# A small load by GpSimd ahead of everything, and two transposing turns placed differently, in a two-matmul kernel with a GELU between

## The chip, the core and the metric

The kernel runs on one core of one Trainium2 chip. The metric is the device time of one execution in microseconds. Before the change three runs gave 117.18, 117.56 and 117.73 us; the median is 117.56.

The engines go by the names of the profile: PE is TensorE (matmuls; PEld is its loading of weights), DVE is VectorE, ACT is ScalarE, POOL is GpSimd, SP is SyncE. SP, ACT and POOL also issue DMA transfers; the profile calls the queue of SP's transfers q1, that of POOL's q0, that of ACT's q10.

## The reference

```python
m, k, n, p = 1024, 1024, 2048, 1024          # a: m x k, b: k x n, c: n x p, all float32

def reference(a, b, c):
    h = np.matmul(a, b)
    h = 0.5 * h * (1 + np.tanh(np.sqrt(2 / np.pi) * (h + 0.044715 * h ** 3)))
    return np.matmul(h, c).astype(np.float32)
```

## The kernel before, in words

**The work.** The kernel computes the first product transposed: a tile of 128 columns of b as weights, the transposed a as the moving operand, so that a result is h transposed (hT, 16 tiles of 128 rows, in two halves of 512 columns: half 0 for the upper 512 rows of a, half 1 for the lower). The first four tiles (columns 0 to 511 of b) are summed over eight steps of 128 along k, both halves side by side. All that remains is done as three groups of block products, seven for each two-by-two product of blocks (`seven`, `product`, line 212): `zero` for columns 512 to 1023 of b, `one` for columns 1024 to 2047, `two` for the second matmul. GELU runs on ACT on the way from PSUM to hT.

**Loads.** SP loads the first pieces in float32 (lines 75 to 79): columns 0 to 255 of a's upper rows (`sta[:, 0, 0]`), rows 0 to 255 of b's first 512 columns (`stb[:, 0:2]`), columns 0 to 255 of a's lower rows (`sta[:, 1, 0]`), columns 256 to 511 of a's upper rows (`sta[:, 0, 1]`), rows 256 to 383 of b (`stb[:, 2]`). DVE and ACT cast these to bf16 (`cast_a`, `cast_b`). POOL loads all the rest with the cast to bf16 in the transfer (lines 91 to 104): the other quarters of a (`abq`, four row tiles by 256 columns), the rest of b, and c. Before the first of these it copies one element per partition of the first piece of a to `gate` (line 81), so that its transfers are issued only after that piece has landed. POOL's transfers use eight completion semaphores in turn: each from the ninth on waits for the one eight before it.

**Turns.** a must be transposed on PE. A turn (line 138) takes one quarter of one half of a, 512 rows by 256 columns. It goes in two parts, one for each 128 columns: four transposes of 128x128 into a half of a PSUM bank, then a DVE copy of 128x512 to `aT` (line 146). As a generator it stops after each part, so that matmuls can be placed between them. Given one bank, both parts use it, and the second part's transposes wait for the first part's copy; given two banks, each part has its own.

**The order of work.** It is written out by hand, and each engine runs its instructions in that order. PE begins with throwaway float32 matmuls (`stir`). Then come the turn of the first upper quarter (0, 0), with the first two steps along k of the upper half (`block(0, ...)`), the turn of the first lower quarter (1, 0), the first two steps of the lower half, the turn (0, 1) and so on, a turn between every two or so blocks, each using what has just landed. The lower half has only three of its four result tiles in that loop, since the banks are taken; the fourth (`ps[1, 3]`, bank 7) is summed after the upper half's end. The last turn, of the last lower quarter (1, 3), stands among the matmuls of this fourth tile. Behind it come steps 6 and 7 of the lower half, then `zero`.

The places that the change touches are lines 51 to 55 (the identity for the transposes, `gate`, `g`, and a tile `room` that nothing uses), lines 237 to 242 (the first lower quarter's cast and turn) and lines 272 to 278 (the fourth tile and the last turn). `cast_a` (line 128) splits a quarter's 256 columns over the engines it is given; a pair in its place casts two row tiles each on the two engines of the pair.

Of the kernel before, what the change touches and what calls it, by code (L numbers as in the profile page):

```python
# [9 lines left out]
F32 = mybir.dt.float32  # L10
# [9 lines left out]
def kernel(ctx, tc, a, b, c, out):  # L20
    nc = tc.nc
    M, K = a.shape
    _, N = b.shape
    _, P = c.shape
# [5 lines left out]
    bv = b.rearrange("(kt p) n -> p kt n", p=128)  # L30
# [3 lines left out]
    consts = ctx.enter_context(tc.tile_pool(name="consts", bufs=1))  # L34
# [5 lines left out]
    def slot(tag, shape, dt, name):  # L40
        return big.tile(shape, dt, name=name, tag=tag)

    def bank(i, shape=(128, H), dt=F32, name="ps"):
        return pp.tile(list(shape), dt, name=name, tag=f"bank{i}", padded_shape=None)

    def pieces(tag, bufs, shape, dt, name):
        return small.tile(shape, dt, name=name, tag=tag, bufs=bufs)

    warm = nc.const_aps.tensor(0.0, [128, 256], F32)
    ident = consts.tile([128, 128], BF16, name="ident")  # L50
    make_identity(nc, ident)
    gate = consts.tile([128, 1], F32, name="gate")
    g = consts.tile([128, 1], F32, name="g")

    consts.tile([128, 16], F32, name="room")

    c_sb = keep.tile([128, NT, P], BF16, name="c_sb")
    hT = [keep.tile([128, NT, H], BF16, name=f"hT{h}") for h in range(2)]
# [8 lines left out]
    abq = slot("x3", [128, 4, 2, 4, 256], BF16, "abq")  # L67
# [31 lines left out]
    for n in range(2):  # L99
        for k in range(0, KT, 4):  # L100
            nc.gpsimd.dma_start(out=b2[:, k:k + 4, ts(n, H)],
                                in_=bv[:, k:k + 4, ds(1024 + n * H, H)])
# [3 lines left out]
    def copy(eng, dst, src):  # L106
        if eng is nc.scalar:
            nc.scalar.activation(dst, src, AF.Copy)
        else:
            nc.vector.tensor_copy(dst, src)  # L110

    def mm1(p, t, h, ks):
        for k in ks:
            nc.tensor.matmul(p, b1[:, k, ts(t, 128)], aT[:, h, k],  # L114
                             start=(k == 0), stop=(k == KT - 1))
# [4 lines left out]
    ps = {(0, t): bank(t) for t in range(4)}  # L120
# [7 lines left out]
    def cast_a(h, q, *engs):  # L128

        ab = pieces("ab", 2, [128, 4, 256], BF16, "ab")  # L130
        for i, eng in enumerate(engs):
            w = 256 // len(engs)
            for j, e in enumerate(eng if isinstance(eng, tuple) else (eng,)):
                m = slice(2 * j, 2 * j + 2) if isinstance(eng, tuple) else slice(0, 4)
                copy(e, ab[:, m, ts(i, w)], sta[:, h, q][:, m, ts(i, w)])
        return ab

    def turn(h, q, i, ab):

        banks = i if isinstance(i, tuple) else (i,)  # L140
        pts = [bank(x, (128, 2, H), BF16, "pt") for x in banks]
        for n in range(2):
            pt = pts[n % len(pts)]
            for m in range(4):
                nc.tensor.transpose(pt[:, n, ts(m, 128)], ab[:, m, ts(n, 128)], ident)  # L145
            nc.vector.tensor_copy(aT[:, h, 2 * q + n], pt[:, n])  # L146
            yield

    def cast_b(k, *engs):
        c0 = 0  # L150
        for i, eng in enumerate(engs):
            w = (H - c0) if i == len(engs) - 1 else H // len(engs) // 128 * 128
            copy(eng, b1[:, k, ds(c0, w)], stb[:, k, ds(c0, w)])
            c0 += w

    def block(h, tiles, ks):
        for k in ks:
            for t in tiles:
                mm1(ps[h, t], t, h, (k,))
# [70 lines left out]
    tn = turn(0, 0, 4, cast_a(0, 0, nc.vector))  # L230
# [3 lines left out]
    next(tn)  # L234
    stir(64)
    cast_b(1, nc.scalar)
    ab = cast_a(1, 0, nc.vector, nc.scalar)
    block(0, range(4), (0,))
    block(0, range(2), (1,))
    for _ in turn(1, 0, (7, 6), ab):  # L240
        pass
    block(0, range(2, 4), (1,))
    ab = cast_a(0, 1, (nc.scalar, nc.vector), nc.vector)
    cast_b(2, nc.scalar, nc.scalar)
    for t in range(3):
# [3 lines left out]
    tn = turn(0, 1, 7, ab)  # L249
# [4 lines left out]
    for q in range(1, 3):  # L254
        k = 2 * q
        block(0, range(4), (k,))
        tn = turn(1, q, 7, abq[:, q, 1])
# [5 lines left out]
        tn = turn(0, q + 1, 7, abq[:, q + 1, 0])  # L263
# [6 lines left out]
    for t in range(4):  # L270
        gelu(t, 0, ps[0, t])
    ps[1, 3] = bank(7)
    mm1(ps[1, 3], 3, 1, range(2))
    tn = turn(1, 3, 0, abq[:, 3, 1])
    next(tn)
    mm1(ps[1, 3], 3, 1, range(2, 5))
    next(tn)
    mm1(ps[1, 3], 3, 1, (5,))
    zero.t[2], x11 = pair(1)
# [208 lines left out]
```

## Time and profile before

| What | Value |
|---|---|
| Runs, us | 117.18, 117.56, 117.73; median 117.56 |
| The profiled execution | 117.6 us, of which the span is 115.8 |
| Granted TensorE clock | 1.0 |
| Busy share of the span | PE 96%, PEld 67%, DVE 78%, ACT 44%, POOL 15% |
| Bytes moved | 15.94 MB by DMA, q0 9.31 MB, q1 6.42 MB |

The span runs from the first to the last instruction of the profiled execution; 1.8 us of that execution's time lie outside it. Times in the text that are given as a moment ("at 8.47") are microseconds from the span's start. A line of the timeline gives start, duration, engine, line of the code, operation, what it writes and reads, how many instructions are merged, and in brackets how long the engine had been idle before and what ended that. A line of the chain of waits gives start, duration and the work or transfer that held up the end at that time. A matmul's duration includes the depth of the pipeline, so consecutive ones overlap: with 512 columns they last 379 ns and start 216 ns apart. In the DMA views each queue has its packets, its megabytes and the time its packets took as a share of sixteen engines over the window.

### The profile page before, as it was taken

Reading aid. Unit: us, or ns where it says so; the run is one execution under the profiler, and the core shown is the slowest. Engines: PE = TensorE matmul, PEld = TensorE weight load, DVE = VectorE, ACT = ScalarE, POOL = GpSimd, SP = SyncE. Lnnn points to the kernel's source line nnn. Section 1 sums busy time; section 2 is a strip of 40 time slices with the busy share of each in tenths; the row PEclk is TensorE's granted clock in tenths of the full one; section 3 lists DMA queues with packets and bytes.
Section 4 is the critical chain, followed back from the end, with each engine's and each line's share of the span. In section 5 each row is a group of like instructions: output and inputs, shape, how many; then the busy total and the mean of one; then the engine's idle time right before and its main releaser. Section 6 shows DMA issues by size and latency. Waiting matters only on the chain.

```text
span 115.8 us, 1473 instructions
## 1 busy us (share of the span) xinstructions
PE 110.7 (96%) x544; PEld 77.1 (67%) x550; DVE 90.1 (78%) x108; ACT 51.4 (44%) x86; POOL 17.3 (15%) x29
## 2 busy tenths in 40 slices
PE   7889999999999999999999999999999999999990
PEld 6545555445777447888886444588888888888870
DVE  0247747689999998944789999999999986964581
ACT  5053000799268998066699339700043992000000
POOL 2497754222332000000000000000000000000000
PEclk9999999999999999999999999999999999999999
DMA  3999999999999999998000000070000002004994
GB/s 74 296 381 221 200 199 204 204 207 207 205 210 210 211 212 212 212 210 163 9 0 0 6 0 0 0 272 0 0 0 0 0 0 94 2 27 173 364 358 166
DMA packets 13414, 15.94 MB, mean 138 GB/s; under 512 B 736, under 2 KB 9184, under 8 KB 13408
## 3 DMA queue, kind: packets, MB, share of 16 engines
q0 software_dynamic: 8672, 9.31, 47.6%
q1 hardware_dynamic: 4592, 6.42, 15.7%
q10 hardware_dynamic: 144, 0.13, 0.3%
q8 instruction: 4, 0.07, 0.2%
q14 instruction: 2, 0.02, 0.0%
HBM read 20.97 MB, written 4.19 MB: 217 GB/s over the span
## 4 chain that ended last, share of the span: by engine, by line
PE 79%; DMA 13%; POOL 5%; issue 0%; DVE 0%
PE ps L212 76%; DMA abq<-in_a_dram 10%; DMA sta<-in_a_dram 3%; POOL abq L86 3%; PE ps L114 2%; POOL b L89 1%; POOL gate L81 1%; PE pt L145 1%; POOL b L92 0%; DVE ot L375 0%
## 5 line engine op out<-in xcount | busy, mean ns | idle before, releaser
L212 PE MATMUL ps<-x,s 128*128 128x512 f32 x128 | 29.6, 391 | 0.0
L212 PEld LDWEIGHTS ps<-x,s 128*128 128x128 f32 x128 | 24.0, 188 | 5.1
L212 PE MATMUL ps<-x,x 128*128 128x512 f32 x96 | 22.9, 394 | 0.0
L212 PEld LDWEIGHTS ps<-x,x 128*128 128x128 f32 x96 | 18.0, 188 | 3.9
L114 PE MATMUL ps<-aT,b 128*128 128x512 bf16 x62 | 15.7, 379 | 0.3 <-DVE b L110 0.2
L298 ACT ACTIVATE v<-ps 128x512 f32<-128x512 f32 x10 | 6.0, 598 | 19.1 <-PE ps L212 19.1
L212 PE MATMUL ps<-c_sb,hT 128*128 128x512 bf16 (+2 forms) x78 | 14.1, 336 | 0.1
L212 PE MATMUL ps<-x 128*128 128x512 f32 x56 | 13.2, 393 | 0.0
L212 PEld LDWEIGHTS ps<-x 128*128 128x128 f32 x56 | 10.2, 188 | 2.7 <-ACT u L298 0.4
L212 PEld LDWEIGHTS <-hT 128*128 128x128 bf16 x80 | 7.1, 98 | 7.0 <-issue 0.5
L118 ACT ACTIVATE hT<-ps 128x512 bf16<-128x512 f32 x14 | 7.3, 596 | 9.6 <-PE ps L114 9.6
L118 ACT ACTIVATE hT<-ot 128x512 bf16<-128x512 f32 x18 | 10.4, 623 | 2.1 <-DVE ot L303 2.0
L146 DVE COPY aT<-pt 128x512 bf16<-128x512 bf16 x16 | 6.7, 422 | 5.5 <-PE pt L145 5.4
L212 PE MATMUL ps<-aT,b 128*128 128x512 bf16 x46 | 10.6, 379 | 0.1
L303 DVE TENSOR_TENSOR ot<-ps,u 128x512 f32<-128x512 f32 x10 | 6.7, 688 | 5.2 <-ACT u L298 5.2
L303 DVE TENSOR_TENSOR ot<-ps,v 128x512 f32<-128x512 f32 x10 | 6.7, 688 | 4.9 <-DMA out_dram<-ot 3.9
L170 DVE TENSOR_TENSOR x<-c_sb 128x1024 fp32r<-128x1024 bf16 x8 | 9.2, 1216 | 0.0
L114 PEld LDWEIGHTS <-b 128*128 128x128 bf16 x64 | 5.7, 97 | 4.5 <-DVE b L110 0.3
L212 PEld LDWEIGHTS <-b 128*128 128x128 bf16 x48 | 4.6, 97 | 5.7 <-issue 0.3
L104 POOL DMA_DIRECT2D c_sb<-in_c_dram x8 | 5.6, 703 | 13.4 <-DMA b<-in_b_dram 11.1
L170 DVE TENSOR_TENSOR x<-b 128x1024 fp32r<-128x1024 bf16 (+1 forms) x4 | 7.0, 1751 | 0.6 <-issue 0.6
L298 ACT ACTIVATE u<-ps 128x512 f32<-128x512 f32 x10 | 5.9, 597 | 3.4 <-PE ps L212 3.2
(44 smaller groups left out, 110.7 us busy)
## 6 DMA issues: line engine op xcount, KB each, us to landing
c_sb<-in_c_dram POOLq DMA_DIRECT2D x8, 512.0 KB, 19.7
out_dram<-ot SPq DMA_DIRECT2D x14, 256.0 KB, 2.1
b<-in_b_dram POOLq DMA_DIRECT2D x6, 512.0 KB, 15.6
sta<-in_a_dram SPq DMA_DIRECT2D x3, 512.0 KB, 6.2
abq<-in_a_dram POOLq DMA_DIRECT2D x5, 256.0 KB, 8.0
stb<-in_b_dram SPq DMA_DIRECT2D x1, 512.0 KB, 5.4
b<-in_b_dram POOLq DMA_DIRECT2D x2, 256.0 KB, 8.3
stb<-in_b_dram SPq DMA_DIRECT2D x1, 256.0 KB, 7.2
```

Source lines behind the costliest of these rows:

```text
L81: nc.gpsimd.tensor_copy(gate, sta[:, 0, 0, 3, 0:1])
L86: nc.gpsimd.dma_start(out=abq[:, q, h], in_=a_part(h, q))
L89: nc.gpsimd.dma_start(out=b1[:, 2 * q:2 * q + 2, 0:H], in_=b_part(q))
L104: nc.gpsimd.dma_start(out=c_sb[:, t:t + 2], in_=cv[:, t:t + 2])
L114: nc.tensor.matmul(p, b1[:, k, ts(t, 128)], aT[:, h, k], start=(k == 0), stop=(k == KT - 1))
L118: nc.scalar.activation(hT[h][:, t], p, AF.Gelu_apprx_tanh)
L145: nc.tensor.transpose(pt[:, n, ts(m, 128)], ab[:, m, ts(n, 128)], ident)
L146: nc.vector.tensor_copy(aT[:, h, 2 * q + n], pt[:, n])
L170: nc.vector.tensor_tensor(out=dst[:, r], in0=x[:, r], in1=y[:, r], op=op)
L212: nc.tensor.matmul(p[:, ds(c0, w)], l[:, k, ts(j, 128)], r[:, k, ds(c0, w)], start=(start and k == 0), stop=(k == self.kt - 1), skip_group ...
L298: nc.scalar.activation(st, p, AF.Copy)
L303: nc.vector.tensor_tensor(out=ot, in0=p, in1=st, op=ADD)
```

## The change

Three edits.

1. `room` is used: the first thing that POOL does in the kernel's own code is to load 8 float32 values from each of b's rows 0 to 255 into it (two rows per partition). Nothing reads them. The construction of the identity comes after it on POOL. The tile's place among `gate` and `g` changes; the addresses behind them don't.
2. The first lower quarter's cast: the first 128 columns were cast by DVE and the second 128 by ACT. Now the first 128 are cast by both (two row tiles each) and the second 128 by DVE. Its turn, whose eight transposes stood together ahead of two matmuls, goes in two parts: four transposes, a matmul, four transposes, a matmul.
3. The last turn: it stood behind two of the fourth tile's matmuls, with three more between its parts, both in bank 0. Now it stands behind four, with one between its parts, in banks 0 and 1.

The number of instructions of PE is the same; ACT has the same number of casts, DVE one more (smaller pieces), POOL one more transfer.

```diff
     ident = consts.tile([128, 128], BF16, name="ident")
+    room = consts.tile([128, 2, 8], F32, name="room")
+    nc.gpsimd.dma_start(out=room, in_=bv[:, 0:2, 0:8])
     make_identity(nc, ident)
     gate = consts.tile([128, 1], F32, name="gate")
     g = consts.tile([128, 1], F32, name="g")
 
-    consts.tile([128, 16], F32, name="room")
...
-    ab = cast_a(1, 0, nc.vector, nc.scalar)
+    ab = cast_a(1, 0, (nc.vector, nc.scalar), nc.vector)
     block(0, range(4), (0,))
     block(0, range(2), (1,))
-    for _ in turn(1, 0, (7, 6), ab):
-        pass
-    block(0, range(2, 4), (1,))
+    tn = turn(1, 0, (7, 6), ab)
+    next(tn)
+    block(0, (2,), (1,))
+    next(tn)
+    block(0, (3,), (1,))
...
-    mm1(ps[1, 3], 3, 1, range(2))
-    tn = turn(1, 3, 0, abq[:, 3, 1])
-    next(tn)
-    mm1(ps[1, 3], 3, 1, range(2, 5))
+    mm1(ps[1, 3], 3, 1, range(4))
+    tn = turn(1, 3, (0, 1), abq[:, 3, 1])
+    next(tn)
+    mm1(ps[1, 3], 3, 1, (4,))
     next(tn)
     mm1(ps[1, 3], 3, 1, (5,))
```

## The prediction

> **What bounds the kernel now.** I read the page's shares first, then the chain of waits in order of time, then the timeline up to 27 us, and last the DMA queues in short windows.
>
> The page, parts 1 and 4:
>
> ```profile
> PE 110.7 (96%) x544; PEld 77.1 (67%) x550; DVE 90.1 (78%) x108; ACT 51.4 (44%) x86; POOL 17.3 (15%) x29
> PE 79%; DMA 13%; POOL 5%; issue 0%; DVE 0%
> ```
>
> TensorE is the bound. After the first real matmul (6.90 us) it hardly stands still, so what an edit can win is the sum of the small holes before that and shortly after it. The chain says which wait ends last there:
>
> ```profile
> 9.52 0.64 POOL b L89
> 10.15 11.43 DMA abq<-in_a_dram
> 21.58 0.05 issue
> 21.63 0.40 PE pt L145 x4
> 22.02 0.65 PE ps L114 x3
> 22.67 0.25 PE pt L145 x4
> ```
>
> The last quarter of a's lower rows, issued at 10.15, lands at 21.58; the last turn waits for it. The timeline gives the size of that hole and of those round the first lower turn:
>
> ```profile
> 7.99 0.43 DVE L110 CAST ab<-sta 128x512 bf16<-128x512 f32 x1 [0.68 <-DMA sta<-in_a_dram]
> 7.99 0.63 ACT L108 ACTIVATE ab<-sta 128x512 bf16<-128x512 f32 x1 [0.44 <-DMA sta<-in_a_dram]
> 8.47 0.62 PE L145 MATMUL pt<-ident,ab 128*128 128x128 bf16 x8
> 8.91 0.76 DVE L146 COPY aT<-pt 128x512 bf16<-128x512 bf16 x2 [0.49 <-PE pt L145]
> 8.93 1.26 PE L114 MATMUL ps<-aT,b 128*128 128x512 bf16 x5
> ...
> 19.16 2.32 PE L114 MATMUL ps<-aT,b 128*128 128x512 bf16 x10
> ...
> 21.62 0.23 PEld L145 LDWEIGHTS <-abq 128*128 128x128 bf16 x4 [0.64 <-DMA abq<-in_a_dram]
> ```
>
> Ten matmuls of 379 ns in 2.32 us start (2.32 - 0.38)/9 = 0.216 us apart. The tenth starts at 21.10, the next could at 21.32, the transposes start at 21.63: a hole of 0.31 us. The page's idle time hides most of it, because matmul ends overlap.
>
> Last the queues, in the windows 5.1 to 8.8 and 8.8 to 10 us:
>
> ```profile
> DMA packets 1201, 1.33 MB, mean 359 GB/s; under 512 B 46, under 2 KB 1060, under 8 KB 1201
> q1 hardware_dynamic: 1201, 1.33, 103.7%
> ```
> ```profile
> q0 software_dynamic: 270, 0.14, 93.3%
> q1 hardware_dynamic: 92, 0.14, 31.4%
> ```
>
> q1 carries SyncE's loads, q0 GpSimd's. GpSimd's first load was issued from 5.14 to 6.02, yet q0 moves nothing before 8.8 and takes over as q1 runs dry. The DMA engines are full from 2 us on, so any added DMA work before 22 us pushes all that follows it.
>
> **The change, part by part.** One profiled execution is the base: 117.6 us (span 115.8, 1.8 around it), 0.04 above the median of 117.56.
>
> *The last turn.* Two matmuls move ahead of it: TensorE now comes to it at 21.32 + 2 x 0.216 = 21.75, after 21.58. The hole of 0.31 goes. What is late next: four transposes (0.22), one matmul, four transposes, one matmul, so block row 6 asks for its operand 0.88 after the turn begins. VectorE's copy begins 0.43 after the transposes (21.63 to 22.06), lasts 0.42 and is seen 0.05 later: 0.90. A hole of about 0.03 opens. The halves now go to banks 0 and 1: GELU releases both by 20.44 + 2 x 0.52 = 21.5, and the next user of bank 1 comes after 24.7. Net -0.28. It can't be much more: the second product wants the other half of b's second column block at about 26.4, less than 0.3 after it lands at 26.2.
>
> *The first lower turn.* The first half's cast goes to both engines. Two of four row tiles cost VectorE 0.28 and ScalarE 0.42 (the same shapes at 9.58 and 9.48), so it is ready at 7.99 + 0.42 = 8.41 instead of 8.42: nothing won, ScalarE is last now. VectorE alone does the second half, 0.43 to 0.68 (both durations occur for that shape), done by 8.7 to 8.9. One matmul now stands between the transposes, so the second four start at 8.90 instead of 8.71 and VectorE's second copy at about 9.34 instead of 9.25. That copy heads VectorE's queue of casts and copies up to the second transposes of the next turn (10.93), which wait for the previous copy: +0.09. Behind them everything on TensorE moves by that. Bounds: 0 if VectorE has room, +0.2 if all of the 0.19 is passed on; nearest is 0.09.
>
> *The new load's issue.* 256 rows, as line 89's: 0.73 (bounds 0.55 of line 92 and 0.88 of the first line 86). ident's memset and select (0.20, 0.29) move from 0.74 to about 1.5 and end at 2.0. TensorE first needs ident at 5.21, GpSimd's next work is at 4.49: hidden by 2.4 us at least; without that cover it would cost 0.73. On GpSimd's queue each load past the eighth waits for the one eight before (line 98 at 11.63 for the first abq); now the last lower quarter waits for the new load, which must land by 10.15. Even if not, the queue ahead of that quarter is long.
>
> *The new load's packets.* 256 of 32 bytes, 16 an engine. No such packet is in the trace. By the packet records semaphore writes of 4 bytes take 9 to 22 ns, rows of 1 KB 44 ns: 0.14 to 0.70 us of each engine. I take 20 ns, near the small ones: 0.32. Up to 2.4 us the engines have gaps (the window 2 to 3.7 shows q1 at 24 GB/s for several slices), so I let half of it fall there: +0.16 on q1 if early, on q0 if it has to wait for 8.8. On q1 it shifts all loads and so all of TensorE; on q0 the tightest arrival is the lower rows' third quarter, landed 15.95 and used at 16.02. Below nothing too: q0's first packets at 8.82 took 327 to 508 ns against 60 later, which an earlier first use could take away, and SyncE's first load of b, over the same 256 rows, runs slowly: 277 GB/s in 3.7 to 5.9, 386 in 5.9 to 8.7. If the touch cured that, its 0.52 MB would land 0.52/277 - 0.52/386 = 0.5 us earlier. Ends for this part: -0.5 and +0.7; I take +0.16, nearest the packet rows.
>
> The Trainium skill speaks against this load (DMA: Bandwidth & Descriptors, Specifications): below 512 B a DMA engine does a read-modify-write. No row here shows what that costs; twice the packet time would make the sum 0.16 worse. The same page (Queues, rings and completion order) says that an engine goes round its queues packet by packet. The windows above differ: for 2.8 us after its first issue ended q0 got no turn beside q1. I go by the trace; the rule would give the second rival's time.
>
> Sum: -0.28 + 0.09 + 0.16 = -0.03, so 117.6 - 0.03 = 117.57, or 117.53 on the median's scale. I say 117.5.
>
> **The rivals.** About 0.5% (0.59 us) is what a measurement of this kernel can tell from no change.
>
> 1. *The small packets come first and are dear.* They stand ahead of SyncE's first loads; each engine is held for 16 x 44 ns = 0.70 plus one slow first packet of 0.4 as at 8.82: 1.1, all of it in front of everything. 117.6 - 0.19 + 1.1 = 118.5. It decides from 0.78 of delay on. For it: the first load sits on the chain (0.74 to 4.44). Against: SyncE issues at the same 0.74 with 0.42 of work, GpSimd needs 0.73.
> 2. *A queue once woken takes turns.* If the 2.8 us of silence is q0's first use and not q1's precedence, q0 starts near 7 and halves q1. SyncE's third load of a, 0.55 MB away from done at 7.0, needs 2.9 us instead of 1.45 and lands 1.4 late; the turn at 10.03 waits. The hole at 21.32 then is gone without help: 117.6 + 1.4 - 0.3 = 118.7; half of it 118.2. For it: the slow first packets. Against: the packet records show three engines finishing q1 at full pace (2 KB in 80 ns) up to 9.5, while q0 runs on others. It decides when abq's packets start before 8.
> 3. *The touch speeds up b's first load.* -0.5 - 0.19: 116.9. For it: the same rows, 277 against 386 GB/s. Against: SyncE's later load of other rows of b, just as new, ran 2 KB in 80 ns untouched.
> 4. *The new load does nothing early:* it waits behind q1 until 8.8 and only delays q0 by 0.14 to 0.3. 117.4 to 117.7, inside the forecast.
>
> **How the numbers follow.** Forecast with case 4: 0.64, range 117.1 to 118.0. Case 1: 0.10. Case 2: 0.11. Case 3: 0.15. So faster 0.15, same 0.64, slower 0.21. The range leaves out the far ends of cases 1 and 2 and some of case 3: 116.9 to 118.4.
>
> **What the profile after would show.** The wait of TensorE's weight load for abq at 21.62 gone or under 0.2, ten matmuls become twelve before it. First lower turn at 8.46 in two groups of four, VectorE's copies 0.34 or more apart, the next turn's second transposes near 11.0. A POOL load at 0.74, ident done near 2.0. SyncE's first landing (4.44) and TensorE's first real matmul (6.90) later by under 0.3. q0 silent between the new load and about 8.8. I am wrong if 6.90 moves by more than 0.4 either way (case 1 or 3), if q0's abq packets mix with q1's before 8 (case 2), or if the instruction fetch seen on q8 in 19 to 21.6, which holds one engine about 1 us (2.3% of 16 engines over 2.6 us), falls otherwise and the last quarter lands well before or after 21.6.

## The result, and the profile after

The kernel after takes 117.74 us (median of 15 runs, 117.53 to 118.09), the kernel before beside it 117.33 us (15 runs, 117.15 to 117.75): a ratio of 1.0035, 95% interval 1.0024 to 1.0047. It is slower by 0.41 us. That is inside the 0.5% that the prediction counts as no change and inside its range, but the forecast was 0.03 us to the other side. The profiled execution took 117.83 us with a span of 116.1. Ten of before's fifteen executions took 117.15 to 117.45 us and five 117.56 to 117.75; the profiled one, at 117.6, is like the five.

The page's shares and the engines of the chain that ended last, after:

```profile
PE 111.2 (96%) x544; PEld 77.7 (67%) x550; DVE 90.4 (78%) x109; ACT 51.1 (44%) x86; POOL 18.1 (16%) x30
PE 89%; DMA 6%; SPq 1%; DVE 1%; issue 0%
```

PE is the bound as before. What has changed is the wait by which the chain comes to PE: POOL's 5% are gone, and so is abq's transfer. The chain of waits in order of time, after:

```profile
1.77 6.68 DMA sta<-in_a_dram
8.45 0.02 issue
8.47 0.53 DVE ab L111
9.00 0.05 issue
9.05 0.40 PE pt L146 x4
...
19.90 2.59 PE ps L115 x12
22.49 0.22 PE pt L146 x4
```

The end is now set by SP's third load (a's first lower quarter), issued at 1.77 and landed at 8.45; from its cast on, PE hardly stands still. The chain before came to PE by the last lower quarter, which landed at 21.58. The timeline, after, shows the same two places and GpSimd's new load:

```profile
1.25 0.84 POOL L52 DMA_DIRECT2D room<-in_b_dram  x1 [0.80 <-POOLq L475]
...
2.38 0.29 POOL masks.py:199 TENSOR_SCALAR_AFFINE_SELECT ident<-ident 128x128 bf16<-128x128 bf16 x1
...
8.47 0.42 ACT L109 ACTIVATE ab<-sta 128x256 bf16<-128x256 f32 x1 [0.88 <-DMA sta<-in_a_dram]
8.47 0.85 DVE L111 CAST ab<-sta 128x256 bf16<-128x256 f32 x2 [1.06 <-DMA sta<-in_a_dram]
9.05 0.40 PE L146 MATMUL pt<-ident,ab 128*128 128x128 bf16 x4 [0.58 <-DVE ab L111]
9.50 0.39 PE L146 MATMUL pt<-ident,ab 128*128 128x128 bf16 x4
...
19.74 2.75 PE L115 MATMUL ps<-aT,b 128*128 128x512 bf16 x12
22.33 0.39 PE L146 MATMUL pt<-ident,abq 128*128 128x128 bf16 x4
```

PE waits 0.58 us at the first lower turn by this line, which counts from the end of the last matmul. By the starts of the matmuls, the prediction's measure, it stands 0.74 us (the last begins at 8.09, the next could at 8.31, the transposes begin at 9.05). Before it stood 0.27 there too (7.99, 8.21 and 8.47), hidden by the overlap: SP's third load was the last thing waited for in both profiles, and what delays it delays PE. The turn's start moves by 0.58. At the last turn there is no wait any more: twelve matmuls, and the transposes 2.59 us (12 times 0.216) after the first of them. The first matmul of `zero` starts at 24.96 instead of 24.70: +0.58 at the first lower turn, less the hole of 0.31 at the last, is +0.27, and the span is 0.3 longer.

Where the 0.58 comes from is in the DMA windows. The window 5.1 to 8.8, which the prediction shows of before, and the shorter one 5.4 to 6.6, first before:

```profile
DMA packets 372, 0.41 MB, mean 345 GB/s; under 512 B 16, under 2 KB 324, under 8 KB 372
q1 hardware_dynamic: 372, 0.41, 104.4%
```

and after, first 5.1 to 8.8, then 5.4 to 6.6:

```profile
DMA packets 1070, 1.11 MB, mean 300 GB/s; under 512 B 48, under 2 KB 999, under 8 KB 1070
q1 hardware_dynamic: 1038, 1.10, 87.2%
q0 software_dynamic: 32, 0.01, 16.5%
...
DMA packets 193, 0.20 MB, mean 163 GB/s; under 512 B 31, under 2 KB 156, under 8 KB 193
q0 software_dynamic: 31, 0.01, 50.7%
q1 hardware_dynamic: 162, 0.19, 48.1%
```

Each line of a queue has its packets, megabytes and share of sixteen engines. The new load's packets carry 8 KB and fill half of the window: 50.7% of 1.2 us is 0.61 us of every engine. By the packet records they are sixteen of 512 B, by their number one for each engine with its sixteen rows together, 400 to 830 ns each, and they start at 5.41 to 6.33, behind SP's second load and ahead of its third. In that window q1 moves 0.19 MB instead of 0.41; at 345 GB/s the missing 0.22 MB are 0.64 us. By the landing events SP's third load lands at 8.45 instead of 7.97, the fourth at 9.78 instead of 9.37, the fifth at 10.62 instead of 10.07, and the first abq at 11.84 instead of 11.34.

### The profile page after: what moved, and what is told of

The parts are those of the page before. It is cut to its first block, busy times and chain, and to the rows that moved or that the text cites. A ratio compares the mean times of both kernels' runs of the same rounds, so it can differ in the third digit from the quotient of the medians.

```text
span 116.1 us, 1475 instructions
## 1 busy us (share of the span) xinstructions
PE 111.2 (96%) x544; PEld 77.7 (67%) x550; DVE 90.4 (78%) x109; ACT 51.1 (44%) x86; POOL 18.1 (16%) x30
## 4 chain that ended last, share of the span: by engine, by line
PE 89%; DMA 6%; SPq 1%; DVE 1%; issue 0%
PE ps L213 76%; PE ps L115 11%; DMA sta<-in_a_dram 6%; PE pt L146 3%; DVE ab L111 0%; SPq L77 0%; SPq L76 0%; DVE ot L378 0%
```

## The experiments

Eighteen kernels beside the kernel before, on the same chip in each group, before between 117.26 and 117.29 us. The kernels that leave out an edit have before's code there; none leaves out work. Times are medians, ratios have their 95% interval. Where an expectation names a theory by a letter, the text behind it says which it is.

### Each edit by itself

`room_only` has edit 1 alone (the load), `first_only` edit 2 (the first lower turn), `last_only` edit 3 (the last turn), `no_room` edits 2 and 3. Their diffs against before are the parts of the change's diff.

```diff
# room_only
+    room = consts.tile([128, 2, 8], F32, name="room")
+    nc.gpsimd.dma_start(out=room, in_=bv[:, 0:2, 0:8])
     make_identity(nc, ident)
...
-    consts.tile([128, 16], F32, name="room")
# first_only
-    ab = cast_a(1, 0, nc.vector, nc.scalar)
+    ab = cast_a(1, 0, (nc.vector, nc.scalar), nc.vector)
...
# last_only
-    mm1(ps[1, 3], 3, 1, range(2))
-    tn = turn(1, 3, 0, abq[:, 3, 1])
+    mm1(ps[1, 3], 3, 1, range(4))
+    tn = turn(1, 3, (0, 1), abq[:, 3, 1])
...
# no_room: first_only and last_only together
```

> The kernel before with only the new load in front. Theory A (the new load's packets hold each DMA engine for some 0.6 us between SyncE's second and third load): the third load of a lands about 0.45 us later, TensorE's first lower turn with it, and the hole of 0.31 before the last turn closes because TensorE is late: +0.1 to +0.25 us net, 1.001 to 1.002. Theory B (the split cast and turn cost it): no difference, 0.999 to 1.001.

> The kernel before with only the first lower quarter's cast and turn split. Theory A: VectorE's later copies make TensorE 0.1 to 0.2 us late near 11 us, and the hole of 0.31 before the last turn takes that up: 0 +- 0.1 us, 0.999 to 1.001. Theory B: the split alone makes the kernel slower by 0.3 to 0.4 us, 1.0025 to 1.0035.

> The kernel before with only the last turn two matmuls later, in two banks. Both theories: the hole of 0.31 us before the last turn goes, a hole of 0.03 opens behind it: -0.28 us, 0.9976; if the last quarter's landing at 21.6 was an accident of one execution, 0.

> The changed kernel without the new load. Theory A: -0.28 for the last turn, +0.1 to +0.2 for the split: -0.1 to -0.2 us against the kernel before, 0.998 to 0.999; so the load is worth 0.5 to 0.6 us of the changed kernel's time. Theory B: as slow as the changed kernel, 1.002 to 1.004.

| Kernel | us | ratio to before |
|---|---|---|
| room_only | 117.80 | 1.0038 [1.0018, 1.0058] |
| first_only | 117.30 | 0.9991 [0.9970, 1.0011] |
| last_only | 117.22 | 0.9994 [0.9974, 1.0013] |
| no_room | 117.30 | 0.9999 [0.9981, 1.0018] |

The load is the whole of the loss (1.0038 and 0.9999 together are 1.0037, the change is 1.0035), and the two turns are worth nothing that can be measured, with intervals of 0.2% on either side. room_only loses more than the 0.1 to 0.25 us that was expected; the expectation let the delay close the hole of 0.31 before the last turn. That hole is the surprise: it stood on before's chain, and yet the timeline of first_only, in which the last turn stands as before, has none:

```profile
19.11 2.32 PE L114 MATMUL ps<-aT,b 128*128 128x512 bf16 x10
21.05 0.42 PEld L145 LDWEIGHTS <-abq 128*128 128x128 bf16 x4
21.27 0.39 PE L145 MATMUL pt<-ident,abq 128*128 128x128 bf16 x4
```

Ten starts 0.216 apart from 19.11 on bring PE to 21.27, and there the transposes start. By the landing events the quarter had landed on all sixteen DMA engines by 19.90. In before's profiled execution fifteen had landed by 19.92 and the sixteenth at 21.58: a 16 KB packet of the instruction queue, started at 19.57, had held that engine for 0.97 us. The semaphore write that stood behind it started at 20.57; the other fifteen had started by 19.56. The queues of before in the window 19 to 21.6 show the packet:

```profile
q0 software_dynamic: 565, 0.52, 124.0%
q8 instruction: 1, 0.02, 2.3%
```

first_only has it too, in the window 19 to 21.3:

```profile
q8 instruction: 1, 0.02, 2.6%
```

So the hole is not in every execution. The fetch is in all twenty profiles, 0.97 us long each time; in first_only it also starts at 19.57, in room_late 0.04 us after the quarter's last semaphore write. Only in before did it come ahead of one of the quarter's writes on its engine, and of the seventeen profiles with the last turn in its old place only before's has the hole. How often it comes is not shown. The profiled execution, at 117.6 us, is 0.27 above the median of 117.33 of the fifteen runs.

### The load's place

`room_late` issues the load behind the loads of c, as POOL's last. `room_gate` issues it behind the gate, ahead of the first abq (the tile in its old place in both).

```diff
# room_late
     for t in range(0, NT, 2):
         nc.gpsimd.dma_start(out=c_sb[:, t:t + 2], in_=cv[:, t:t + 2])
+    nc.gpsimd.dma_start(out=room, in_=bv[:, 0:2, 0:8])
# room_gate
+    nc.gpsimd.dma_start(out=room, in_=bv[:, 0:2, 0:8])
     cast_load_a(1, 1)
```

> Only the new load, issued by GpSimd last of all its loads, behind c. Its packets then come when TensorE no longer waits for loads. Both theories: 0 +- 0.1 us, 0.999 to 1.001; a difference would say that the tile or the extra instruction costs by itself.

> Only the new load, issued behind the gate copy at about 5, just ahead of GpSimd's first quarter. Order of arrival (A3) and fixed delay (A4) agree: its packets come near 8.8, behind SyncE's loads, which land as before; GpSimd's loads land 0.3 to 0.6 later, and TensorE first waits at the third lower quarter (used at 16.0): +0.2 to +0.5 us, 1.002 to 1.004. If only loads in front of SyncE's are dear: 0.

room_late took 117.30 us, 1.0010 [0.9997, 1.0022]: at the end the load costs nothing that can be told. room_gate took 117.85 us, 1.0052 [1.0034, 1.0070], which was not to be expected from its packets: by the packet records they took 27 ns each, at 8.8 to 9.5, and q1 in the window 5.4 to 6.6 is as full as before. The timeline and the waits of PEld between 8 and 27 us show where its time went instead:

```profile
12.55 1.04 PE L115 MATMUL ps<-aT,b 128*128 128x512 bf16 x4 [0.28 <-DMA b<-in_b_dram]
...
PEld L146 <- DMA abq<-in_a_dram: 0.5, 1, 0.5
PEld L115 <- DMA b<-in_b_dram: 0.5, 1, 0.5
```

Later transfers of q0 landed late. The packet records have four slow packets between 11.19 and 11.73 (264, 264, 276 and 434 ns), and by the landing events one DMA engine of the sixteen was some 0.65 late with the load that landed next and with those behind it. Why is open, and so is what this place costs when that does not happen.

### When q0's packets are served

With issue ending at 2.09 and packets at 5.41, the load either waits in order of arrival behind what SP had issued by then (A3), or some fixed time after its issue (A4). `room_held` makes SP's second load wait for a write by POOL that stands behind the new load, so that this load is issued ahead of SP's second.

```diff
# room_held: room_only, and
     nc.sync.dma_start(out=sta[:, 0, 0], in_=a_part(0, 0))
+    nc.gpsimd.memset(stb[:, 0:2, 0:1], 0.0)
     nc.sync.dma_start(out=stb[:, 0:2], in_=b_part(0))
```

> The new load, with SyncE's second load made to wait for a small GpSimd memset behind it, so that SyncE's second to fifth load are issued after it, from about 2.4 on. Order of arrival (A3): the new load's packets come behind the first load alone, at 3.5 to 4.0, before b's first rows. Fixed delay from GpSimd's issue to its first packet (A4): at 5.2 to 5.6 as before, among the later loads. The time itself, some 0.5 to 2 us longer by the held loads, tells nothing.

It took 121.28 us, 1.0344 [1.0313, 1.0375], as SP's loads come later. The timeline, and the queues in the window 3.55 to 4.5:

```profile
2.62 0.10 POOL L77 MEMSET stb<- 128x2 f32 x1
2.74 0.38 SPq L78 DMA_DIRECT2D stb<-in_b_dram  x1
...
q1 hardware_dynamic: 91, 0.10, 57.8%
q0 software_dynamic: 31, 0.01, 10.5%
```

SP's second load is issued at 2.74, and now the load's packets start at 3.63 to 4.03, straight behind SP's first load, and most of them take 27 ns (10.5% of 0.95 us is 0.10 us an engine, semaphore writes included). So the order of arrival decides, not a fixed delay. And the packets are not dear by their nature, nor as q0's first: here they are q0's first too.

The Trainium skill (DMA: Bandwidth & Descriptors, Queues, rings and completion order) says that an engine goes round its queues packet by packet. No run here shows such turns: the load was served whole behind what had been issued before it, at 3.63 or at 5.41, and before's first q0 packets, issued by 6.02, came at 8.82. The same page (Specifications) lets a DMA engine do a read-modify-write below 512 B. Sixteen rows of 32 B, a packet of 512 B, in 27 ns show no price for it, and neither do the packets of 256 B of the second load of `room_twice` below, most of which took 25 ns.

### Rows, bytes, and two loads

`room_128`, `room_512` and `room_wide` change the shape at the same place, `room_twice` loads the same bytes in two. A1 is a price by the row; against it stands a price by the packet or by the place.

```diff
# room_128: 128 rows of 64 B
+    nc.gpsimd.dma_start(out=room, in_=bv[:, 0, 0:16])
# room_512: 512 rows of 16 B
+    nc.gpsimd.dma_start(out=room, in_=bv[:, 0:4, 0:4])
# room_wide: 256 rows of 128 B, tile [128, 2, 32]
+    nc.gpsimd.dma_start(out=room, in_=bv[:, 0:2, 0:32])
# room_twice: two loads of 256 rows of 16 B
+    nc.gpsimd.dma_start(out=room[:, :, 0:4], in_=bv[:, 0:2, 0:4])
+    nc.gpsimd.dma_start(out=room[:, :, 4:8], in_=bv[:, 0:2, 4:8])
```

> Only the new load, with its 8 KB as 128 rows of 64 bytes (8 an engine instead of 16). Theory A1 (each row costs an engine some 40 ns whatever its size): q0's first packets last about 0.3 us instead of 0.4 to 0.85, half the loss: +0.2 us, 1.002. Theory A2 (one fixed price for the first transfer of GpSimd's queue): as with 256 rows, +0.45 us, 1.004.

> Only the new load, with its 8 KB as 512 rows of 16 bytes (32 an engine). Theory A1: the packets last about 1.2 us, +0.9 to +1.1 us, 1.008 to 1.009. Theory A2: +0.45 us, 1.004.

> Only the new load, with 256 rows of 128 bytes, four times the bytes in the same number of rows; the tile is 192 bytes per partition longer. Theory A1 and A2: as with 32 bytes, +0.45 us, 1.004. Were it the bytes, the packets would last four times as long and the loss be well over 1 us.

> Only the new load, as two loads of 256 rows of 16 bytes one after the other. If the price is one of the first use of GpSimd's queue: +0.45 us, 1.004, and the second load's packets short (under 0.1 us). If every such load pays: 32 packets of 0.3 to 0.6 us before 8.6, +0.8 to +1.0 us, 1.007 to 1.0085.

| Kernel | us | ratio to before | mean packet, ns |
|---|---|---|---|
| room_128 | 117.71 | 1.0045 [1.0024, 1.0066] | 309 |
| room_only | 117.80 | 1.0038 [1.0018, 1.0058] | 560 |
| room_512 | 117.80 | 1.0051 [1.0034, 1.0068] | 468 |
| room_wide | 118.34 | 1.0095 [1.0079, 1.0111] | 701 (2 KB) |
| room_twice | 117.93 | 1.0058 [1.0039, 1.0076] | 380 to 1020, then mostly 25 |

Four times the rows cost the same within the intervals, so A1 falls. Nor does the packets' mean length set the loss: room_128's are about half as long as room_only's, yet SP's third load lands at 8.39 against 8.42. The profiled executions roughly follow that landing: 117.25 us with 7.88 (room_late), 117.72 with 8.39 (room_128), 118.13 with 8.74 (room_512), 118.45 with 9.11 (room_wide). In room_twice the second load's packets come at 7.2 to 8.5, between SP's third and fourth load, and nearly all are short. That would fit a price of the first load only; but room_held's packets are a first load too, and short. What is left is what stands beside them.

### The tile's address, without and with the load

Edit 1 also moves the tile in SBUF, and room_wide makes it longer. `room_oldplace` issues the load first of all but keeps every address; `wide_tile` and `pad512` have only a longer tile that nothing uses (256 and 192 bytes per partition instead of 64).

```diff
# room_oldplace: ident, gate, g, then
+    room = consts.tile([128, 2, 8], F32, name="room")
+    nc.gpsimd.dma_start(out=room, in_=bv[:, 0:2, 0:8])
+    make_identity(nc, ident)
# wide_tile, no load
+    consts.tile([128, 2, 32], F32, name="room")
# pad512, no load
+    consts.tile([128, 48], F32, name="room")
```

> The kernel before with nothing but the unused tile 192 bytes per partition longer, as the load of 128-byte rows had it. If the 1.08 us of that run are its packets: no difference, 0.999 to 1.001. If the shifted addresses cost: 1.002 to 1.005, and the packets the rest.

> The new load first of all on GpSimd, but with its tile where the unused tile stood before, so that no address changes. If the load's packets cost the time: as with the tile moved, +0.4 to +0.5 us, 1.004, packets of 0.3 to 0.85 us between 4.8 and 6.8. If the moved tile costs it: no difference.

> The kernel before with nothing but the unused tile made 192 bytes per partition instead of 64. If only the place of the large tiles modulo some power of two matters (192 bytes more cost 0.43 us), this shift of 128 bytes gives another time than the kernel before, either way, by 0.1 to 0.5 us; if the earlier difference was an accident of that run, 0.999 to 1.001.

room_oldplace took 117.92 us, 1.0059 [1.0037, 1.0080], its packets 549 ns: the load costs without any address moved. wide_tile took 117.79 us, 1.0037 [1.0023, 1.0051], and pad512 117.50 us, 1.0021 [1.0006, 1.0035], with no instruction changed. In their profiles SP's third load lands at 8.10 and 8.09, against 7.72 to 7.97 in before, first_only, last_only, no_room, room_late and room_gate. By the packet records the 2 KB packets of SP's last load took 93 ns in both instead of 84, but 91 in room_only too, which shifts no large tile. So of room_wide's 0.95% about 0.37% is the tile and 0.6% its packets, if the two add. Why an address costs time is open.

### What the rows are

If the packets are slow because SP's second load is reading the same rows of b at that time (C1), the same load from elsewhere is cheap. `room_far` reads b's rows 768 to 1023, `room_c` 256 rows of c.

```diff
# room_far
+    nc.gpsimd.dma_start(out=room, in_=bv[:, 6:8, 0:8])
# room_c
+    nc.gpsimd.dma_start(out=room, in_=cv[:, 8:10, 0:8])
```

> The new load from rows 768 to 1023 of b instead of 0 to 255, at the same pitch. C1 (the packets are slow because SyncE's second load reads the same rows at that moment): packets of 27 to 100 ns as where the load stood alone, 0 to +0.15 us, 1.000 to 1.001. C2 (packets of many short rows are slow whenever the engines are at b's rows, whichever): 0.4 to 0.85 us a packet, +0.45 us, 1.004.

> The new load from rows 1024 to 1279 of c, another tensor with half the pitch. C1: as with the far rows of b, 0 to +0.15 us. C2 with b's pitch as the cause: short packets too, while the far rows of b are slow. C2 with any short rows: +0.45 us, 1.004.

The queues in the window 5.4 to 6.6, of room_only:

```profile
q1 hardware_dynamic: 160, 0.20, 51.8%
q0 software_dynamic: 25, 0.01, 33.7%
```

of room_far:

```profile
q1 hardware_dynamic: 353, 0.39, 96.7%
q0 software_dynamic: 32, 0.01, 3.0%
```

and of room_c:

```profile
q1 hardware_dynamic: 249, 0.28, 71.6%
q0 software_dynamic: 32, 0.01, 20.0%
```

With other rows of b the packets stand in the same place, 5.5 to 6.13, and all sixteen take 27 ns; q1 moves 0.39 MB as before does (0.41). With c they take 115 to 340 ns, mean 231. The times follow: room_far 117.55 us, 1.0018 [1.0006, 1.0030]; room_c 117.64 us, 1.0026 [1.0013, 1.0038]; room_only 1.0038. Rows that are not just being read make the packets cheap. SP's third load lands at 7.87 with the far rows, at 8.17 with c and at 8.42 in room_only. That c lies between says that being the same rows is not all of it; what else makes the packets slow is open. And room_far's 0.18%, with packets of 27 ns, has no cause that these runs show.

### Is SP's second load itself the victim?

SP's second load runs slowly even before (240 to 270 GB/s in 3.7 to 5.4). If its shape, two blocks of 128 rows in one transfer, is the reason (D1), two transfers should be quicker: `split_b` by rows, `split_cols` by columns.

```diff
# split_b
-    nc.sync.dma_start(out=stb[:, 0:2], in_=b_part(0))
+    nc.sync.dma_start(out=stb[:, 0], in_=bv[:, 0, 0:H])
+    nc.sync.dma_start(out=stb[:, 1], in_=bv[:, 1, 0:H])
# split_cols
+    for c0 in (0, 256):
+        nc.sync.dma_start(out=stb[:, 0:2, c0:c0 + 256], in_=bv[:, 0:2, c0:c0 + 256])
```

> The kernel before with SyncE's second load (rows 0 to 255 of b, which ran at 240 to 270 GB/s between 3.7 and 5.4) as two loads of 128 rows. D1 (the slow stretch comes from reading two blocks of rows, 1 MB apart, side by side; the 128-row load at 8.5 to 9.5 takes 84 ns for 2 KB): the stretch runs at 330 GB/s or more, everything behind lands about 0.3 us earlier, -0.2 to -0.3 us, 0.9975 to 0.9985. D2 (the stretch is slow for another reason): 0 +- 0.1 us, or 0.1 to 0.2 us slower for the added issue.

> The same load as two loads of 256 columns each, all 256 rows in both (rows of 1 KB). D1: no gain, the two blocks are still read side by side, 0 to +0.2 us. If shorter rows alone helped: the stretch faster, -0.2 us.

Both are slower: split_b 119.67 us, 1.0176 [1.0147, 1.0206]; split_cols 118.89 us, 1.0135 [1.0108, 1.0163]. In split_b q1 moved 167 GB/s in 3.7 to 5.4. The queue in the window 3.7 to 8.3 and the first wait on the timeline, of split_b, and then the queue of no_room, whose loads are before's:

```profile
q1 hardware_dynamic: 907, 1.12, 88.0%
...
9.17 0.60 PE L115 MATMUL ps<-aT,b 128*128 128x512 bf16 x2 [1.37 <-ACT b L109]
```
```profile
q1 hardware_dynamic: 1226, 1.46, 101.8%
```

D1 falls: 0.34 MB less in 4.6 us, and PE waits 1.37 us for b. The loss is also far above the 0.2 us that D2 allowed. Why this load is slow stays open, and so does whether the same cause makes the new load's packets slow.

No kernel tried beats before by more than its interval.

## Why the prediction was right or wrong

**The time.** 117.5 with 116.9 to 118.4 was said and 117.74 came; by the ratio the change costs 0.41 us where the sum said -0.03. That the time lies within 0.24 of 117.5 is in part luck: the base was one execution of 117.6, and before's median is 117.33. Two of the three terms were wrong, in ways that do not cancel.

**The last turn: "The hole of 0.31 goes ... Net -0.28".** In the profiled execution it does go. At the median there was nothing like it to win: last_only is 0.9994, though its interval just takes in -0.28 (0.9976), and none of the other sixteen profiles with the old order has the hole. The step that failed is taking a wait of one execution as a wait of the kernel. The prediction saw the sign of it, the instruction fetch on q8, and named it as a reason to be wrong, yet put the hole into the sum at its full size. The sixteen landing events of before would have told: 19.92 on fifteen, 21.58 on one. In the profile after, the quarter lands at 20.34, well before the turn; with that, one of the prediction's own signs of being wrong came true.

**The first lower turn: "+0.09".** first_only is 0.9991 with an interval of 0.2% on either side: 0.09 us (0.08%) is not refuted and not seen. One thing that the working left out showed in a profile: in the profile after DVE's half of the first cast took 0.53 us where the working had 0.28, some 0.1 of the 0.58 at 9.05 (0.48 is the later landing).

**The new load's issue.** Right as hidden. Its start was off: 1.25 to 2.09 instead of 0.74, ident done at 2.67 instead of 2.0, needed by PE at 5.44.

**The new load's packets: "I take 20 ns ... half of it fall there: +0.16".** This is the term that decides. room_only measures +0.45 us (0.38% of 117.26), within the ends of -0.5 and +0.7. Its parts were wrong both in size and in place: not 256 small packets but sixteen of 512 B; not 0.32 us of each engine but 0.60; and neither in the gaps before 2.4 nor from 8.8 on, but at 5.41 between SP's second and third load. SP's later loads and the first abq land 0.41 to 0.55 later, and PE waits for the third load. That a delay on q1 shifts all of TensorE was right. The step that failed is pricing the packets as if nothing were read beside them: by themselves most take 27 ns (room_held), less than the 0.32 us of the sum.

**The rivals.** The first (dear packets in front of everything) comes nearest: dear they are, but behind SP's first two loads, so that SP's first landing moved only from 4.44 to 4.67 and the first real matmul from 6.90 to 7.01, under the 0.3 that the forecast allowed. The second (the queue takes turns once woken) falls: abq's packets start at 9.49 and do not mix with q1's before 8; the order of arrival decides. The third (the touch speeds up b's load) is wrong in sign: with b's rows read beside SP's load of them the change loses. The fourth (the load waits behind q1 until 8.8) is wrong in place, 5.41; the silence of q0 before 8.8 was not precedence of q1 but that SP's loads had been issued earlier.

**The points to look for.** Right: twelve matmuls and no wait at the last turn, two groups of four at the first lower turn, first landing and first real matmul. Wrong: the first lower turn near 8.46 (9.05), the next turn's second transposes near 11.0 (11.51), and q0's silence from the new load to 8.8 (its packets were themselves at 5.4 to 6.8).

## What to carry to other kernels

Before a hole of one profiled execution goes into a sum, see whether that execution stands above the median by about the hole's size, and look at the sixteen landing events of the late transfer. One engine late by itself may not come again: here one of seventeen profiles has the hole. A second profile of the same kernel, or of one that leaves the place alone, tells more than the first. A small transfer is priced by its place in the order of issue over all queues and by what it reads beside, not by its bytes: the same 8 KB cost 0.45 us among the first loads, and nothing that could be told at the end. (Behind the gate they cost 0.5% with packets of 27 ns, for a reason left open.) An early load that nothing needs early belongs behind those that PE waits for, and if it has to stand there, its source should not be rows that a neighbour is reading.

## What the runs showed of the hardware

- Transfers issued by different engines were served in the order of issue (3.63, 5.41 and 8.82 for q0's first packets, by what SP had issued before).
- Sixteen rows of 32 B went as one packet of 512 B on each DMA engine: mostly 27 ns by itself, 27 ns from other rows of b, 231 ns from c, 550 to 600 ns from the rows that SP's load was reading.
- An instruction fetch of 16 KB held one DMA engine for 0.97 us in every profile; in one the semaphore write of a load stood behind it, and that load landed at 21.58 instead of 19.92.
- 192 or 128 bytes more of an unused tile cost 0.37% and 0.21% (intervals from 0.23% and 0.06%).
- Splitting one load of 256 rows of b in two cost 1.8% by rows and 1.35% by columns.
